# Token norm of a chunked scan: sums from one product with ones, and the power taken of 256 columns on every partition

## The chip, the cores and the metric

One core of one Trainium2 chip runs the program alone. The metric is the device time of one execution in microseconds (us), the median of several runs on the chip. A profiled execution gives the durations of single instructions.

## The reference, cut to what matters

The program is one residual layer of 256 tokens and 2048 channels: one input projection, a Mamba-2 scan and an attention branch on its results, two branch projections, a gated sum and an output projection. The part that the change touches is the gated group norm at the end of the scan branch. For each of 4 groups of 512 channels, with `y` the scan's output:

```python
y = y.reshape(bsz, L, SSM_D_INNER) * jax.nn.silu(z.astype(jnp.float32))
yg = y.reshape(bsz, L, SSM_GROUPS, -1)
yg = yg * lax.rsqrt(jnp.mean(yg * yg, axis=-1, keepdims=True) + EPS)
y = yg.reshape(bsz, L, SSM_D_INNER) * gn_m.astype(jnp.float32)
```

So each token has, in each group, one sum of squares over 512 channels, and one inverse root that scales all 512.

## The kernel before, in words

The projections keep TensorE busy. Their weights come in chunks of 1 MB: a DMA on SP's queue brings `raw`, ScalarE rounds it to `hi` (line 130), VectorE subtracts to get `lo` (line 131), and TensorE multiplies with both. Three chunks are held at once, and two are fetched ahead of the one in use (`next_chunk`): when TensorE begins chunk i, `hi` and `lo` of chunk i+2 are written into the buffers that chunk i-1 has just left. A chunk of the transposed kind (`chunk_t`, lines 159 and 164) is 16 products of 512 columns with `hi` and 16 of 256 columns with `lo`; within it two of the one kind and two of the other alternate, and the first product with `lo` stands third.

The scan works on channels as partitions and tokens as columns. Per group the program projects B and C, then x, then z (10 chunks), with the scan's own steps laid between the chunks by `after(n, fn)`, which runs `fn` n chunks later. The steps at the end of group g run during the first chunks of the next group, or, for the last group, during the projection of the indexer's queries:

- `mix` (lines 441 to 468) forms the gated output `yt` and, in `sz[:, 0, :]`, for each of 128 partitions the sum of 4 squares per token. The sum over the partitions is missing.
- `token_norm` (lines 470 to 481), two chunks later: TensorE takes each half of the squares as weights and a column of ones as the moving operand, which puts the sums of 128 tokens on 128 partitions, one column per half (`prs`, line 474). VectorE scales and adds the epsilon (line 476). GpSimd raises to the power -0.5 (line 477), on 128 partitions and 2 columns. ScalarE multiplies the identity with the two columns (line 480), which gives two diagonal matrices `dgy`.
- `normalised_y` (lines 483 to 496), two chunks after that: TensorE multiplies ones with the diagonals, which lays the factors along the columns on every partition (`prt`, line 487). VectorE multiplies four blocks of `yt` by the norm weight and by `prt` (line 490), ScalarE rounds to `yh`, VectorE subtracts to `yl`. The branch projection that reads `yh` and `yl` comes after the indexer.

The pool of small products in PSUM has 4 buffers (`aux_tile`). The pools `grp` and `grp2` of SBUF hold `dgy` in one buffer and `ss` in two. The order of the instructions on each engine is not the order of the source: the program's scheduler places them by readiness and priority, and each engine then executes its list strictly in order. `decay` (line 406) is the neighbour in time: lines 412, 418, 421 and 426 on VectorE, 409 and 410 on TensorE.

Of the kernel before, what the change touches and what calls it, by code (L numbers as in the profile page):

```python
# [11 lines left out]
F32 = mybir.dt.float32  # L12
F32R = mybir.dt.float32r
AF = mybir.ActivationFunctionType
ALU = mybir.AluOpType
# [3 lines left out]
P = 128  # L19
T = 256  # L20
D = 2048
KB = 16
EPS = 1e-6
# [9 lines left out]
PN, PCW, PCB, PGN, PDS, PDT, PAL = 0, 16, 112, 136, 152, 168, 169  # L33
# [51 lines left out]
def block_kernel(ctx, tc, W, w0, xT, xn, par, gbias, nf, out):  # L85
    nc = tc.nc
    mm = nc.tensor.matmul
# [14 lines left out]
    def aux_tile(shape, name):  # L102
        return paux.tile(shape, F32, tag="aux", name=name)
# [117 lines left out]
    part = const.tile([P, NPAR], F32, name="part")  # L221
    nc.sync.dma_start(part, par)
    ones = const.tile([P, P], F32, name="ones")
    nc.gpsimd.memset(ones, 1.0)
    mhalf = const.tile([P, 2], F32, name="mhalf")
    nc.gpsimd.memset(mhalf, -0.5)
    ident = const.tile([P, P], F32, name="ident")
# [17 lines left out]
    for k0, k1 in PIECES:  # L245
# [8 lines left out]
        for k in range(k0, k1):  # L254
            g = part[:, PN + k:PN + k + 1]
# [11 lines left out]
    grp = ssm.enter_context(tc.tile_pool(name="grp", bufs=1))  # L267
    grp2 = ssm.enter_context(tc.tile_pool(name="grp2", bufs=2))
# [200 lines left out]

    def token_norm(sz):  # L470

        prs = aux_tile([P, 2], "prs")
        for tb in range(2):
            mm(prs[:, tb:tb + 1], sz[:, 0, tb * P:tb * P + P], ones[:, 0:1], start=True, stop=True)
        ss = grp2.tile([P, 2], F32, tag="ss", name="ss")
        nc.vector.tensor_scalar(ss, prs, 1.0 / 512.0, EPS, ALU.mult, ALU.add)
        nc.gpsimd.tensor_tensor(ss, ss, mhalf[:, 0:2], op=ALU.pow)
        dgy = grp.tile([P, T], F32, tag="dgy", name="dgy")
        for tb in range(2):
            nc.scalar.activation(dgy[:, tb * P:tb * P + P], ident, AF.Copy, scale=ss[:, tb:tb + 1])  # L480
        return dgy

    def normalised_y(g, yt, dgy):
        prt = aux_tile([P, T], "prt")
        for tb in range(2):
            ts = slice(tb * P, tb * P + P)
            mm(prt[:, ts], ones, dgy[:, ts], start=True, stop=True)
        for b in range(4):
            k = 4 * g + b
            nc.vector.scalar_tensor_tensor(yt[:, b, :], yt[:, b, :], part[:, PGN + k:PGN + k + 1], prt,  # L490
                                           ALU.mult, ALU.mult)
        for a in range(2):
            bs = slice(2 * a, 2 * a + 2)
            ks = slice(4 * g + 2 * a, 4 * g + 2 * a + 2)
            nc.scalar.activation(yh[:, ks, :], yt[:, bs, :], AF.Copy)
            nc.vector.tensor_sub(yl[:, ks, :], yt[:, bs, :], yh[:, ks, :].bitcast(F32))
# [19 lines left out]
    for g in range(4):  # L516
# [17 lines left out]
        sz = grp.tile([P, 4, T], F32, tag="sz", name="sz")  # L534
# [8 lines left out]
        def finish(g=g, M=M, xdt=xdt, xss=xss, sz=sz):  # L543
            yt = mix(g, M, xdt, xss, sz)
            dgy = []
            after(2, lambda: dgy.append(token_norm(sz)))
            after(4, lambda: normalised_y(g, yt, dgy[0]))
# [304 lines left out]
```

## Time and profile before

| what | value |
|---|---|
| median of 3 runs | 1136.45 us (1135.76 to 1136.47) |
| the profiled execution's own time | 1137.44 us |
| its span, from the first to the last instruction | 1135.7 us |
| TensorE busy | 1124.4 us, 99% |
| VectorE busy | 779.5 us, 69% |
| ScalarE busy | 560.5 us, 49% |
| GpSimd busy | 8.8 us, 1% |
| mean granted TensorE clock | 0.999 |

The span and what lies around it (1.7 us) make the profiled time, which is 1.0 us above the median of the runs. Busy shares are averages over the span. A line of the timeline tells the start, the duration, the engine, the source line, the operation, what it writes and reads, and in brackets how long the engine had been idle and what ended that.

### The profile page before, as it was taken

To read this page: it belongs to the slowest core of one execution; us is meant where nothing else is said; L and a number is where in the kernel's file an instruction comes from. 1 tells how busy PE (TensorE), PEld (TensorE's weight loads), DVE (VectorE), ACT (ScalarE), POOL (GpSimd) and SP (SyncE) were. 2 spreads that over 40 slices of the span, in tenths; PEclk is the share of its full clock that TensorE was granted. 3 is DMA by queue.
4 is the path that set the end of the run, shared out by engine and by line. 5 is a ranking of instruction groups with operands and counts; after the bars stand their busy time and mean duration, and the time that the engine had idled before them with its cause. 6 is when DMAs were issued, how large, how long until landed. Compare 5 with 4: busy or idle time off the path is not lost.

```text
span 1135.7 us, 14327 instructions
## 1 busy us (share of the span) xinstructions
PE 1124.4 (99%) x5906; PEld 957.6 (84%) x5906; DVE 779.5 (69%) x995; ACT 560.5 (49%) x532; POOL 8.8 (1%) x24
## 2 busy tenths in 40 slices
PE   9999999999999999999999999999999999999997
PEld 8878888888888888888888888888888888888886
DVE  5788797879777854444447767876678454789663
ACT  6657574849454433334335454555445444333441
POOL 0000000000000000000000000000000000000000
PEclk9999999999999999999999999999999999999999
DMA  8766555563544655555554455445444557555652
GB/s 298 295 217 230 181 189 186 186 222 126 209 148 168 202 205 205 194 190 206 203 188 169 165 185 186 167 147 205 174 161 184 195 197 255 190 220 185 208 199 74
DMA packets 34113, 219.08 MB, mean 193 GB/s; under 512 B 3744, under 2 KB 3968, under 8 KB 9088
## 3 DMA queue, kind: packets, MB, share of 16 engines
q1 hardware_dynamic: 31248, 209.16, 51.9%
q10 hardware_dynamic: 2800, 9.01, 2.3%
q8 instruction: 46, 0.75, 0.3%
q14 instruction: 19, 0.16, 0.0%
HBM read 215.96 MB, written 2.13 MB: 192 GB/s over the span
## 4 chain that ended last, share of the span: by engine, by line
PE 94%; DMA 3%; DVE 2%; ACT 1%; SPq 0%; issue 0%; POOLq 0%; DVEq 0%; POOL 0%; ACTq 0%
PE acc_t L159 30%; PE acc_t L164 15%; PE acc_n L204 14%; PE acc_n L203 14%; PE acc_n L202 14%; DMA raw<-W 2%; PE py L454 1%; DVE lo L131 1%; PE acc_last L204 1%; PE acc_last L202 1%; PE acc_last L203 1%; PE pl L647 1%; PE po L675 1%; PE pi L564 1%; ACT hi L130 0%; DMA xt<-xn 0%
## 5 line engine op out<-in xcount | busy, mean ns | idle before, releaser
L131 DVE TENSOR_TENSOR lo<-raw,hi 128x2048 fp32r<-128x2048 f32 (+2 forms) x197 | 437.5, 2222 | 244.6 <-ACT hi L130 242.2
L130 ACT ACTIVATE hi<-raw 128x2048 fp32r<-128x2048 f32 (+2 forms) x197 | 366.4, 1861 | 446.1 <-PE acc_n L203 222.3
L159 PE MATMUL acc_t<-xx,hi 128*128 128x512 f32 x1472 | 466.7, 398 | 0.0
L164 PEld LDWEIGHTS acc_t<-xx,lo 128*128 128x128 f32 x1472 | 276.3, 188 | 65.2
L164 PE MATMUL acc_t<-xx,lo 128*128 128x256 f32 x1472 | 289.8, 278 | 0.0
L159 PEld LDWEIGHTS acc_t<-xx,hi 128*128 128x128 f32 x1472 | 224.9, 189 | 2.6 <-issue 1.7
L204 PE MATMUL acc_n<-lo,xx 128*128 128x512 f32 x480 | 187.0, 390 | 1.3 <-DVE lo L131 1.3
L202 PE MATMUL acc_n<-hi,xx 128*128 128x512 f32 x480 | 187.0, 390 | 0.0
L203 PE MATMUL acc_n<-hi,xx 128*128 128x512 f32 x480 | 186.9, 389 | 0.0
L204 PEld LDWEIGHTS acc_n<-lo,xx 128*128 128x128 f32 x480 | 90.1, 188 | 20.7 <-DVE lo L131 2.0
L203 PEld LDWEIGHTS acc_n<-hi,xx 128*128 128x128 f32 x480 | 90.1, 188 | 18.9 <-issue 0.3
L202 PEld LDWEIGHTS acc_n<-hi,xx 128*128 128x128 f32 x480 | 90.1, 188 | 18.5
L202 PE MATMUL acc_n<-hi,yh 128*128 128x512 f32 x256 | 99.6, 389 | 0.0
L203 PE MATMUL acc_n<-hi,yl 128*128 128x512 f32 x256 | 99.6, 389 | 0.0
L204 PE MATMUL acc_n<-lo,yh 128*128 128x512 f32 x256 | 99.6, 389 | 0.0
L202 PEld LDWEIGHTS acc_n<-hi,yh 128*128 128x128 f32 x256 | 48.0, 188 | 10.0
L204 PEld LDWEIGHTS acc_n<-lo,yh 128*128 128x128 f32 x256 | 48.0, 188 | 10.0
L203 PEld LDWEIGHTS acc_n<-hi,yl 128*128 128x128 f32 x256 | 48.0, 188 | 9.9
L667 DVE STREAM_TRANSPOSE pT<-le 32x192 f32<-32x192 f32 x128 | 47.3, 370 | 1.9
L401 DVE SCALAR_TENSOR_TENSOR c<-u,part,c 128x255 f32<-128x255 f32 (+2 forms) x72 | 30.2, 477 | 0.3
L726 DVE STREAM_TRANSPOSE mT<-merged 32x256 f32<-32x256 f32 x64 | 27.9, 436 | 0.8
L159 PE MATMUL acc_start<-xx,hi 128*128 128x512 f32 x64 | 17.7, 415 | 1.2 <-ACT hi L130 1.2
(198 smaller groups left out, 734.3 us busy)
## 6 DMA issues: line engine op xcount, KB each, us to landing
raw<-W SPq DMA_DIRECT2D x188, 1024.0 KB, 4.8
acb<-adr ACTq DMA_DIRECT2D x4, 1024.0 KB, 4.7
raw<-W SPq DMA_DIRECT2D x6, 512.0 KB, 7.4
xt<-xn SPq DMA_DIRECT2D x2, 1024.0 KB, 5.3
gb<-gbias SPq DMA_DIRECT2D x8, 256.0 KB, 3.5
xr<-xn ACTq DMA_DIRECT2D x4, 512.0 KB, 6.0
xraw<-xT SPq DMA_DIRECT2D x3, 512.0 KB, 6.5
raw<-W SPq DMA_DIRECT2D x4, 256.0 KB, 5.3
```

What stands on the lines that cost most here:

```text
L130: nc.scalar.activation(hi, raw, AF.Copy)
L131: nc.vector.tensor_sub(lo, raw, hi.bitcast(F32))
L159: mm(acc[:, cb, :], hv[:, k, cb], ax[:, kk].rearrange("p b t -> p (b t)"), start=kk == 0, stop=False, skip_group_check=True)
L164: mm(acc[:, cb, 0:T], lv[:, k, cb], ax[:, kk, 0, :], start=False, stop=kk == KB - 1, skip_group_check=True)
L202: mm(acc[:, c], ah[:, kk, ts], hv[:, k, c], start=kk == 0, stop=False)
L203: mm(acc[:, c], al[:, kk, ts], hv[:, k, c], start=False, stop=False)
L204: mm(acc[:, c], ah[:, kk, ts], lv[:, k, c], start=False, stop=kk == KB - 1)
L401: nc.vector.scalar_tensor_tensor(c[:, b, sh:], u[:, b, :T - sh], wv[3 - sh], c[:, b, sh:], ALU.mult, ALU.add)
L454: mm(py[r, cb, sb * P:], xdt[:, sb, 64 * h:64 * h + 64], M[a][:, 2 * cb + i, (0, T)[sb]:(T, 384)[sb]], start=cb == 0 and sb == 0, stop=cb ...
L564: mm(pi[2 * cb + i][:, cs[tb]], qi[r, cb, tb * P:tb * P + P], kidx[r, :(P, T)[tb]], start=tb == 0, stop=tb == 1, skip_group_check=True, ti ...
L667: nc.vector.transpose(t[sj, :, :, si], lv[si, :, :, sj])
L726: nc.vector.transpose(tv[sn, :, :, si], mv[si, :, :, sn])
```

## The change

`token_norm` multiplies ones, as weights, with the 256 columns of squares. That one product sums over the partitions and leaves every token's sum on every partition, along the columns, where `normalised_y` needs it. VectorE's scaling and GpSimd's power now run on 128 partitions and 256 columns; the exponent is one column, broadcast. The identity's two copies on ScalarE and the second product are gone, and `normalised_y` reads the factors from SBUF (`rs`) where it read them from PSUM (`prt`). `rs` takes the buffer that `dgy` had.

```diff
     def token_norm(sz):
 
-        prs = aux_tile([P, 2], "prs")
-        for tb in range(2):
-            mm(prs[:, tb:tb + 1], sz[:, 0, tb * P:tb * P + P], ones[:, 0:1], start=True, stop=True)
-        ss = grp2.tile([P, 2], F32, tag="ss", name="ss")
-        nc.vector.tensor_scalar(ss, prs, 1.0 / 512.0, EPS, ALU.mult, ALU.add)
-        nc.gpsimd.tensor_tensor(ss, ss, mhalf[:, 0:2], op=ALU.pow)
-        dgy = grp.tile([P, T], F32, tag="dgy", name="dgy")
-        for tb in range(2):
-            nc.scalar.activation(dgy[:, tb * P:tb * P + P], ident, AF.Copy, scale=ss[:, tb:tb + 1])
-        return dgy
-
-    def normalised_y(g, yt, dgy):
-        prt = aux_tile([P, T], "prt")
-        for tb in range(2):
-            ts = slice(tb * P, tb * P + P)
-            mm(prt[:, ts], ones, dgy[:, ts], start=True, stop=True)
+        prs = aux_tile([P, T], "prs")
+        mm(prs, ones, sz[:, 0, :], start=True, stop=True)
+        rs = grp.tile([P, T], F32, tag="dgy", name="rs")
+        nc.vector.tensor_scalar(rs, prs, 1.0 / 512.0, EPS, ALU.mult, ALU.add)
+        nc.gpsimd.tensor_tensor(rs, rs, mhalf[:, 0:1].to_broadcast([P, T]), op=ALU.pow)
+        return rs
+
+    def normalised_y(g, yt, rs):
         for b in range(4):
             k = 4 * g + b
-            nc.vector.scalar_tensor_tensor(yt[:, b, :], yt[:, b, :], part[:, PGN + k:PGN + k + 1], prt,
+            nc.vector.scalar_tensor_tensor(yt[:, b, :], yt[:, b, :], part[:, PGN + k:PGN + k + 1], rs,
                                            ALU.mult, ALU.mult)
```

## Rows read from the trace of the kernel before

**Rows 1.** The page: busy us (share of the span) and instructions of two engines.
```profile
PE 1124.4 (99%) x5906; PEld 957.6 (84%) x5906; DVE 779.5 (69%) x995; ACT 560.5 (49%) x532; POOL 8.8 (1%) x24
```

**Rows 2.** Windows, one group's period: length, then each engine's busy us, granted clock.
```profile
140.60:201.80 61.20, 61.20 (x374) 53.14 (x373) 51.10 (x63) 40.78 (x41) 1.11 (x2) 1.00 0.54 189
```

**Rows 3.** Timeline of PE around the two products of group 0.
```profile
137.52 0.62 PE L159 MATMUL acc_t<-xx,hi 128*128 128x512 f32 x2
...
138.22 0.50 PE L474 MATMUL prs<-ones,sz 128*128 128x1 f32 x4
...
139.36 0.62 PE L159 MATMUL acc_t<-xx,hi 128*128 128x512 f32 x2
...
150.49 0.61 PE L487 MATMUL prt<-dgy,ones 128*128 128x128 f32 x4
...
151.63 0.63 PE L159 MATMUL acc_t<-xx,hi 128*128 128x512 f32 x2
```

**Rows 4.** Timeline of PE: the nearest product of 256 float32 columns, with one of 128.
```profile
144.23 0.63 PE L159 MATMUL acc_t<-xx,hi 128*128 128x512 f32 x2
144.70 0.60 PE L409 MATMUL pcb<-bc 128*128 128x256 f32 x2
...
145.59 0.63 PE L159 MATMUL acc_t<-xx,hi 128*128 128x512 f32 x2
```

**Rows 5.** Groups of instructions on POOL: line, operation, shapes, count | busy us, mean ns.
```profile
L790 POOL TENSOR_TENSOR rf<-rf,mhalf 128x1 f32<-128x1 f32 x2 | 1.1, 550 | 0.2
...
L287 POOL TENSOR_TENSOR rn<-rn,mhalf 128x2 f32<-128x2 f32 x1 | 0.7, 717 | 0.1
...
L314 POOL MEMSET tri<- 128x384 f32 x1 | 0.4, 421 | 0.0
```

**Rows 6.** Timeline of POOL: the powers of groups 0, 2 and 3.
```profile
140.57 1.08 POOL L477 TENSOR_TENSOR ss<-ss,mhalf 128x2 f32<-128x2 f32 x1 [101.48 <-DVE ss L476]
...
263.01 1.00 POOL L477 TENSOR_TENSOR ss<-ss,mhalf 128x2 f32<-128x2 f32 x1 [60.19 <-DVE ss L476]
322.73 0.69 POOL L477 TENSOR_TENSOR ss<-ss,mhalf 128x2 f32<-128x2 f32 x1 [58.72 <-DVE ss L476]
```

**Rows 7.** Groups on DVE: the nearest operation of 256 columns out of PSUM.
```profile
L373 DVE COPY nat<-pn 128x256 f32<-128x256 f32 x1 | 0.4, 423 | 0.0
```

**Rows 8.** Timeline of DVE behind the scaling of group 0; last line, group 2.
```profile
140.34 0.15 DVE L476 TENSOR_SCALAR ss<-prs 128x2 f32<-128x2 f32 x1
140.41 0.68 DVE L421 TENSOR_TENSOR E<-acb,nat 128x512 f32<-128x512 f32 x1
142.24 2.29 DVE L131 TENSOR_TENSOR lo<-raw,hi 128x2048 fp32r<-128x2048 f32 x1 [1.15 <-ACT hi L130]
145.56 0.56 DVE L412 TENSOR_TENSOR cbt<-pcb,tri 128x384 f32<-128x384 f32 x1 [1.03 <-PE pcb L410]
...
151.13 0.48 DVE L490 SCALAR_TENSOR_TENSOR yt<-yt,part,prt 128x256 f32<-128x256 f32 x1
...
155.56 1.25 DVE L490 SCALAR_TENSOR_TENSOR yt<-yt,part,prt 128x256 f32<-128x256 f32 x3
156.74 2.28 DVE L131 TENSOR_TENSOR lo<-raw,hi 128x2048 fp32r<-128x2048 f32 x1
...
262.79 0.68 DVE L421 TENSOR_TENSOR E<-acb,nat 128x512 f32<-128x512 f32 x1
```

**Rows 9.** Timeline of PE: the first products of the chunk that uses that last `lo`.
```profile
162.44 0.71 PE L159 MATMUL acc_t<-xx,hi 128*128 128x512 f32 x2
```

**Rows 10.** Timeline of DVE behind the scaling of group 3.
```profile
323.72 2.29 DVE L131 TENSOR_TENSOR lo<-raw,hi 128x2048 fp32r<-128x2048 f32 x1 [1.14 <-ACT hi L130]
...
331.36 2.29 DVE L131 TENSOR_TENSOR lo<-raw,hi 128x2048 fp32r<-128x2048 f32 x1 [2.83 <-ACT hi L130]
...
334.28 0.69 DVE L194 TENSOR_TENSOR qi<-qi,rbc 128x512 f32<-128x512 f32 x1
```

**Rows 11.** Timeline of PE: the indexer's products that read that `qi`.
```profile
335.55 1.57 PE L564 MATMUL pi<-kidx,qi 64*128 64x128 f32 x12
```

## The prediction
> **What bounds the kernel now.** I read the page's busy times first: TensorE is busy 99% of the span, VectorE 69%, GpSimd 8.8 us in all [rows 1]. A share over the whole span hides stages, so I next took the windows of one group's period of the scan: in 61.2 us TensorE never pauses, at a granted clock of 1.00 (2.4 GHz), and VectorE works 51.1 us, 83% [rows 2]. Two things follow for the change. A TensorE instruction less in this stage is worth what it occupies there. And VectorE, which executes in order and writes the `lo` half of every weight chunk, has only some 10 us of play in 61: if it is held longer than its lead, TensorE stops. So the timelines of TensorE, GpSimd and VectorE around the norm come next.
>
> **What the change takes from TensorE.** The products with `lo` and `hi` alternate with a period of 0.70 us (137.52 to 138.22). Around `prs` the next period begins 1.14 us later instead (138.22 to 139.36), so the first product of the norm costs 0.44 us; around `prt` it is 150.49 to 151.63, again 0.44 us [rows 3]. Both go: 0.88 us per group. The new product is float32, 128x128 weights, 256 columns. The nearest rows are `pcb`: one product of 256 and one of 128 columns stretch a period from 0.70 to 1.36 us, 0.66 us for 384 columns, so 0.44 us for 256 [rows 4]. Ends: 0.12 us, if it streamed like the split products (0.70 us for 1536 columns), and 0.66 us. I take 0.44. The saving is 0.44 us per group, 1.8 us in four groups (0.9 to 3.0).
>
> **What it takes from ScalarE and adds to VectorE.** Eight identity copies leave ScalarE; TensorE has no pause that they end, so I cost that at nothing. VectorE's scaling grows from 0.15 to about 0.42 us, by the copy of 256 columns out of PSUM [rows 7, 8]; with lines 421 and 131 behind it, and 1.15 us idle before line 131 [rows 8], the 0.27 us disappear. The four products with the factor read SBUF for PSUM: same 256 columns, costed at nothing. PSUM's pool loses a tile per group: no wait. No DMA is added or moved.
>
> **What it adds to GpSimd.** This is the unknown. A power of one column takes 0.550 us, of two 0.717 or, in group 3, 0.69 [rows 5, 6]: the second column adds 0.14 to 0.17 us, about 0.153. If each column costs that, 256 take 0.70 + 254 x 0.153 = 39.6 us (36.0 to 43.1). Ends far away: below, 1.1 ns a column as for the memset of 384 columns in 0.42 us, which makes 1.0 us [rows 5]; above, 0.55 us for each column, 141 us. I take 39.6: it is the only pair of rows that shows this operation at two sizes.
>
> By the Trainium skill, GPSIMD Engine Reference, section 3.1 (elementwise, side by side), a two-input elementwise operation on GpSimd is bounded by its one read port at about 2.6 cycles an element of 1.2 GHz. By that page, as an estimate, 254 more columns would add 0.55 us, and the power would be hidden whole. The trace disagrees: the second column alone costs 0.14 us or more, some 60 times as much, so here the function, not the port, is the price.
>
> **Who waits for it.** Before, the power ran well ahead of its reader: it ended at 141.65, the first line 490 ran at 151.13 [rows 6, 8]. What follows on VectorE is the question. In group 0 the power took 1.08 us, and line 421 (two SBUF inputs) ran beside it until 141.09; in group 2 it took 1.00, with line 421 until 263.47. Both powers end 0.54 to 0.56 us after that operation. In group 3 VectorE was idle, and it took 0.69 [rows 6, 8, 10]. So the power waits for such a VectorE operation, and I take it that the exclusion works both ways: no operation with two SBUF inputs starts during a power. Line 131 is one. A second reason gives the same: the scheduler pulls ready work forward on VectorE (of four consecutive lines 490 one stands at 151.13, three at 155.56 [rows 8]), and without TensorE's `prt` ahead of them they are ready by dependency right behind the power, so one may sit in VectorE's list ahead of line 131.
>
> The Trainium skill's page SBUF — State Buffer, section "Who interferes with whom", says that GpSimd and VectorE share a port pair and that a VectorE instruction with two SBUF inputs contends with a GpSimd one that reads SBUF; whoever starts first holds it for the whole instruction. The rows agree in the one direction they show; the other no row shows. By the page VectorE stands still for the whole power; without that rule the sum would be rival A's.
>
> **The sum, groups 0 to 2.** Line 421 ends at 141.36 (0.27 later), the power 0.55 + 254 x 0.153 = 39.4 us after, at 180.8. The `lo` that started at 142.24 is frozen 38.6 us. Behind it VectorE has its list to work off. The `lo` that ended at 159.02 (156.74 + 2.28) is needed by the chunk whose products start at 162.44, after two products with `hi`, so at 162.9: 3.9 us lead [rows 8, 9]. The 1.03 us of idle time ahead of line 412 are filled too [rows 8]. TensorE loses 38.6 - 3.9 - 1.0 = 33.7 us per group. **Group 3:** the power runs alone from 323.0 to 362.6; the `lo` of 323.72 is frozen 38.9 us, and TensorE's products at 335.55 need the `qi` that VectorE finishes at 334.97. Of the 2.83 us idle ahead of the second `lo` ScalarE's rounding still takes most; I count 1.9 as filled: 37 us [rows 10, 11]. Loss: 3 x 33.7 + 37 = 138.1 us; with the saving, +136.3. On the profiled execution's 1137.44 us that is 1273.7; the median of the runs stands 1.0 lower, so 1272.7, and I say 1273.
>
> Slope 0.139 gives 14 us less, 0.167 14 us more: 1258 to 1287. TensorE's clock is 1.00 wherever the rows look, so none shows what a stop of 30 us does to it. A chunk of eight periods, 5.6 us, at the lower level would take 5.6 us more, at most 22 us in four stops; I cost it at nothing, because right after a stop VectorE's list sets the pace, and keep the end for the range.
>
> **Rival A, the cover holds (0.20).** Power as slow, but VectorE runs freely beside it and stops only at line 490, where that stands now. Then the hold is 151.13 to 180.8, 29.7 us, less the lead of 3.9: 25.8 per group; in group 3 from 335 to 362.6, less about 3.9: 23.7. Sum 101 - 1.8: 1236. For it: no VectorE operation with two inputs is seen waiting for a power. Against: the powers are seen waiting.
>
> **Rival B, the long loop is cheaper than its first columns (0.14).** If four columns are in flight together, 0.04 us a column makes 10.9 us: the freeze is 9.9 us, the loss 5.0 per group and 8 in group 3, +21: 1158. At 0.1 us a column the power takes 26 us, the freeze 25, the loss 3 x 20 + 23 - 1.8: 1218. So 1150 to 1220. Against: the second column does not come cheap behind the first.
>
> **Rival C, not slower (0.14).** The power ends before VectorE needs its result or the port. Either a column costs a few ns (the lower end), or nothing excludes VectorE and the lines 490 stand far enough back in its list; `yt`, which they scale, is only replaced a group's period later. The point from which it decides is 10 us of cover, about 40 ns a column, and 1 us if the port is held. Then only TensorE's saving is left: 1134.7, a gain of 0.16%. With the new product at its lower end, 3.0 us, 0.27%. For it: one column more is a thin sample of a loop of 256. Against: 0.14 us.
>
> A steeper slope than 0.167, up to the 141 us end (about 1680), keeps 0.04. The forecast has 0.48.
>
> **How the numbers follow.** The predicted time is the forecast's, 1273; its own range 1258 to 1295 with some of the clock. Range: forecast 0.48, rival A 0.20, rival B above 1160 0.11 give 0.79: 1160 to 1300. A measurement can tell about 0.2% (2.3 us) here. Slower by more: forecast, A, B, steeper, 0.86. Within: most of C, 0.11. Faster: C with the cheap product, 0.03.
>
> **What would show it.** GpSimd's busy time should rise from 8.8 us to about 160, in four powers of 36 to 43 us. VectorE should show one wait per group that ends with the power, ahead of a `lo` near 142 (forecast) or ahead of line 490 near 151 (rival A); TensorE should show idle time in four places of 30 us or more, released by line 131, and none elsewhere; its period around `prs` should be 1.14 us, with no `prt`. Powers under 10 us would make the forecast wrong at its first step; powers of 40 us without idle TensorE, at its second.

## The result and the profile after

The changed kernel takes 1289.44 us (4 runs, 1289.17 to 1290.37) against 1136.46 us: a ratio of 1.1347, 95% interval 1.1333 to 1.136. It is 153 us slower. The profiled execution took 1290.37 us, with a span of 1288.6 us.

Busy times and the clock line of the changed kernel's page; each digit of a row is the busy share, or the granted clock, of a slice of 32 us.

```profile
span 1288.6 us, 14270 instructions
...
PE 1131.8 (88%) x5882; PEld 961.2 (75%) x5882; DVE 780.4 (61%) x995; ACT 558.1 (43%) x524; POOL 170.4 (13%) x24
...
PE   8999629729719808999999999999999999999997
...
POOL 0000660660570570000000000000000000000000
PEclk9999959959959958999999999999999999999999
```

TensorE's busy time rose by only 7 us against [rows 1]; its share fell from 99% to 88%. So most of the loss is waiting. TensorE waits in four places, in the slices in which GpSimd works, and there the clock drops too. VectorE and ScalarE do about the same work as before.

The waits of the changed kernel, who waited for whom, total us, times, longest us:

```profile
DVE yt L482 <- POOL rs L476: 164.4, 4, 41.3
...
PE acc_t L164 <- DVE lo L131: 103.5, 4, 34.3
...
PE pi L556 <- DVE qi L194: 41.5, 1, 41.5
```

Line 476 is the power and line 482 the product with the factor (477 and 490 before). VectorE stands four times for the whole power, and TensorE for VectorE: three times 34 us (and once 0.5), and 41.5 us in group 3. That is 145 us of the 153; the rest comes from the clock, as shown below. In the chain that ended last GpSimd now holds 13%, where it had 0%.

The powers on GpSimd's timeline, and the same two places on VectorE's and TensorE's as in [rows 8] and [rows 3], all of the changed kernel:

```profile
140.25 41.53 POOL L476 TENSOR_TENSOR rs<-rs,mhalf 128x256 f32<-128x256 f32 x1 [100.76 <-DVE rs L475]
...
432.88 41.12 POOL L476 TENSOR_TENSOR rs<-rs,mhalf 128x256 f32<-128x256 f32 x1 [55.25 <-DVE rs L475]
```

```profile
139.75 0.42 DVE L475 TENSOR_SCALAR rs<-prs 128x256 f32<-128x256 f32 x1
140.08 0.68 DVE L421 TENSOR_TENSOR E<-acb,nat 128x512 f32<-128x512 f32 x1
181.81 0.88 DVE L482 SCALAR_TENSOR_TENSOR yt<-yt,part,rs 128x256 f32<-128x256 f32 x2 [41.05 <-POOL rs L476]
182.61 2.28 DVE L131 TENSOR_TENSOR lo<-raw,hi 128x2048 fp32r<-128x2048 f32 x1
```

```profile
136.95 0.63 PE L159 MATMUL acc_t<-xx,hi 128*128 128x512 f32 x2
...
137.65 0.59 PE L473 MATMUL prs<-sz,ones 128*128 128x256 f32 x2
...
138.77 0.63 PE L159 MATMUL acc_t<-xx,hi 128*128 128x512 f32 x2
...
149.97 0.63 PE L159 MATMUL acc_t<-xx,hi 128*128 128x512 f32 x2
184.95 0.80 PE L164 MATMUL acc_t<-xx,lo 128*128 128x256 f32 x2 [34.35 <-DVE lo L131]
185.54 1.05 PE L159 MATMUL acc_t<-xx,hi 128*128 128x512 f32 x2
...
189.19 0.62 PE L159 MATMUL acc_t<-xx,hi 128*128 128x512 f32 x2
```

Read from the bottom: TensorE stops in front of the first product with `lo` of a chunk. That `lo` starts on VectorE at 182.61. In [rows 8] it followed line 421; now two of lines 482 stand between, and the first of them waits for the power. In the order of the list, two of the four lines 482 were drawn ahead from behind the second `lo` to right behind line 421.

Windows of the changed kernel around the first stop; the columns are the stretch and its length, busy us of PE, PEld, DVE, ACT, POOL, then granted clock, DMA share and GB/s:

```profile
150.60:184.90 34.30, 0.00 (x0) 0.00 (x0) 3.09 (x4) 0.00 (x0) 31.18 (x1) 0.56 0.00 0
184.90:189.20 4.30, 4.25 (x15) 3.68 (x16) 4.26 (x7) 0.02 (x1) 0.00 (x0) 0.53 0.68 244
189.20:193.50 4.30, 3.83 (x23) 3.05 (x22) 4.30 (x4) 3.92 (x5) 0.00 (x0) 1.00 0.71 240
...
140.25:238.30 98.05, 63.24 (x368) 54.12 (x367) 51.31 (x63) 40.26 (x39) 41.54 (x2) 0.83 0.33 119
```

The last row is one group's period: 98.05 us in place of 61.20 [rows 2], with the same products on TensorE but for those of the norm. The granted clock fell in the stop and was still at the lower level, 1.2 GHz, in the 4.3 us behind it. ScalarE and the DMA are at 0 in the stop as well: the whole pipeline of weights stands while that one wait lasts.

### The profile page after: what moved, and what is told of

The parts are those of the page before. It is cut to its first block, busy times and chain, and to the rows that moved or that the text cites. A ratio compares the mean times of both kernels' runs of the same rounds, so it can differ in the third digit from the quotient of the medians.

```text
span 1288.6 us, 14270 instructions
## 1 busy us (share of the span) xinstructions
PE 1131.8 (88%) x5882; PEld 961.2 (75%) x5882; DVE 780.4 (61%) x995; ACT 558.1 (43%) x524; POOL 170.4 (13%) x24
## 4 chain that ended last, share of the span: by engine, by line
PE 76%; POOL 13%; DVE 7%; DMA 2%; ACT 1%; issue 1%; SPq 0%; POOLq 0%; DVEq 0%; ACTq 0%
PE acc_t L159 23%; POOL rs L476 13%; PE acc_n L204 12%; PE acc_n L203 12%; PE acc_n L202 12%; PE acc_t L164 11%; DVE lo L131 3%; DMA raw<-W 2%; DVE c L401 1%; ACT hi L130 1%; PE acc_last L204 1%; PE acc_last L203 1%; PE acc_last L202 1%; PE py L454 1%; PE pl L639 1%
## 5 line engine op out<-in xcount | busy, mean ns | idle before, releaser
L159 PE MATMUL acc_t<-xx,hi 128*128 128x512 f32 x1472 | 472.5, 403 | 0.0
L164 PEld LDWEIGHTS acc_t<-xx,lo 128*128 128x128 f32 x1472 | 280.1, 191 | 172.0 <-DVE lo L131 105.6
L164 PE MATMUL acc_t<-xx,lo 128*128 128x256 f32 x1472 | 293.6, 281 | 103.5 <-DVE lo L131 103.5
L159 PEld LDWEIGHTS acc_t<-xx,hi 128*128 128x128 f32 x1472 | 228.6, 192 | 2.7 <-issue 1.7
L476 POOL TENSOR_TENSOR rs<-rs,mhalf 128x256 f32<-128x256 f32 x4 | 165.5, 41378 | 269.0 <-DVE rs L475 269.0
L482 DVE SCALAR_TENSOR_TENSOR yt<-yt,part,rs 128x256 f32<-128x256 f32 x16 | 7.3, 480 | 164.4 <-POOL rs L476 164.4
L398 ACT ACTIVATE c<-u,part 128x256 f32<-128x256 f32 x24 | 13.2, 594 | 121.9 <-DVE u L395 121.8
```

The costliest lines, as they stand in the source:

```text
L159: mm(acc[:, cb, :], hv[:, k, cb], ax[:, kk].rearrange("p b t -> p (b t)"), start=kk == 0, stop=False, skip_group_check=True)
L164: mm(acc[:, cb, 0:T], lv[:, k, cb], ax[:, kk, 0, :], start=False, stop=kk == KB - 1, skip_group_check=True)
L398: nc.scalar.activation(c[:, b, :], u[:, b, :], AF.Identity, bias=part[:, PCB + blk:PCB + blk + 1], scale=wv[3])
L476: nc.gpsimd.tensor_tensor(rs, rs, mhalf[:, 0:1].to_broadcast([P, T]), op=ALU.pow)
```

## The experiments

Two theories stood against each other. T: a column of the power costs 0.16 us, and the loss comes from where its reader stands in VectorE's list. L, the first of the prediction's two reasons for VectorE's stop: a running power keeps out every VectorE operation with two SBUF inputs, so the loss would come wherever the reader stood.

**Everything but the power.** The changed kernel, with

```diff
-        nc.gpsimd.tensor_tensor(rs, rs, mhalf[:, 0:1].to_broadcast([P, T]), op=ALU.pow)
+        nc.gpsimd.tensor_tensor(rs[:, 0:2], rs[:, 0:2], mhalf[:, 0:2], op=ALU.pow)
```

> The power is taken of 2 of the 256 columns; the other columns are multiplied with the mean square itself, so the norm is left out for them. All else is the changed kernel. Theory T (the loss is the length of the power times its place in VectorE's list) and rival L (a running power keeps out every VectorE operation with two SBUF inputs) agree: a power of about 0.7 us, VectorE's wait ahead of line 482 under 1.5 us, no idle TensorE in the scan, and only the saving of the two products left: before less 1.8 us, 1134.7 us (1133.5 to 1136). If the time stays over 1140, something other than the power is slow.

Measured: 1135.34 us, ratio 0.9988 (0.9979 to 0.9997). The powers take 0.69 to 1.08 us as before. So the product with ones, the longer scaling on VectorE and the reader in SBUF together gain about 1 us of the 1.8 expected, at the edge of what can be told. One part of the expectation missed: TensorE does stop in the scan, for 1.1 us in group 3. All of the loss of 153 us is the power's. The page, VectorE's timeline in group 0 and TensorE's in group 3:

```profile
PE 1121.3 (99%) x5882; PEld 954.2 (84%) x5882; DVE 780.8 (69%) x995; ACT 558.6 (49%) x524; POOL 8.7 (1%) x24
```

```profile
140.29 0.68 DVE L421 TENSOR_TENSOR E<-acb,nat 128x512 f32<-128x512 f32 x1
141.57 0.88 DVE L482 SCALAR_TENSOR_TENSOR yt<-yt,part,rs 128x256 f32<-128x256 f32 x2 [0.60 <-POOL rs L476]
142.37 2.29 DVE L131 TENSOR_TENSOR lo<-raw,hi 128x2048 fp32r<-128x2048 f32 x1
```

```profile
334.75 1.58 PE L556 MATMUL pi<-kidx,qi 64*128 64x128 f32 x16 [1.12 <-DVE qi L194]
```

VectorE's list is the changed kernel's: two of lines 482 stand right behind line 421 with a power of 2 columns as with one of 256.

**A long power that nobody reads.** The kernel before, with one line behind line 477 (`base` is a constant tile of 0.7, `spare` a tile of its own):

```diff
         nc.gpsimd.tensor_tensor(ss, ss, mhalf[:, 0:2], op=ALU.pow)
+        nc.gpsimd.tensor_tensor(spare, base, ss[:, 0:1].to_broadcast([P, T]), op=ALU.pow)
```

> The kernel before, with one more power per group on GpSimd, right behind the one of 2 columns: 256 columns into a tile that nobody reads. Nothing waits for its result, so it shows whether a long power holds VectorE by itself. T: the power takes 38 to 45 us, VectorE runs on beside it, and the time is that of before, 1136.5 us (1135 to 1139). L: the lo of each group near 142, 203, 265 and 324 us is frozen to the end of the power, TensorE stops four times for 30 us or more, 1255 to 1290 us.

Measured: 1136.76 us, ratio 1.0002 (0.9992 to 1.0011): nothing lost, with 41 us of power in each group. Its timelines of GpSimd and of VectorE, and a window over the power:

```profile
140.37 41.13 POOL L481 TENSOR_TENSOR spare<-base,ss 128x256 f32<-128x256 f32 x1
```

```profile
140.88 2.29 DVE L131 TENSOR_TENSOR lo<-raw,hi 128x2048 fp32r<-128x2048 f32 x1 [1.14 <-ACT hi L130]
...
145.27 1.75 DVE L429 TENSOR_TENSOR E<-E,cbt 128x1536 f32<-128x1536 f32 x1
...
147.54 2.29 DVE L131 TENSOR_TENSOR lo<-raw,hi 128x2048 fp32r<-128x2048 f32 x1
```

```profile
140.60:182.00 41.40, 41.40 (x244) 36.37 (x243) 34.33 (x37) 28.00 (x29) 40.91 (x1) 1.00 0.57 205
```

The `lo` of 140.88 starts half a microsecond into the power, and 34 us of VectorE's work, lines 131 and 429 with their two SBUF inputs among it, lie beside it, at the durations of before (2.29 us a `lo`, in [rows 8] 2.28 and 2.29). The power is no longer for it either: 41.13 us here, 41.12 in group 3 of the changed kernel, where VectorE stood still. L is refuted.

**The same power, its reader late.** The changed kernel, with

```diff
     def normalised_y(g, yt, rs):
+        prt = aux_tile([P, T], "prt")
+        mm(prt, ident, rs, start=True, stop=True)
...
-            after(4, lambda: normalised_y(g, yt, dgy[0]))
+            after(10, lambda: normalised_y(g, yt, dgy[0]))
```

and `prt` for `rs` in the four products.

> The changed kernel with its power of 256 columns, but its reader comes late: normalised_y runs 10 chunks behind mix instead of 4, and reads the factors through a product with the identity, so that nothing of it can be drawn ahead on VectorE. T: the powers still take 41 us each, all of it beside VectorE and TensorE; the product added is worth the 0.44 us per group that the change saved, so 1136.5 us (1134 to 1140, some waiting where the late steps meet the next mix). L: as slow as the changed kernel, 1270 to 1290 us, with line 131 waiting for GpSimd.

Measured: 1135.96 us, ratio 0.9997 (0.9988 to 1.0006). The powers still take 41 us; the scaling ahead of them stands where it did, and the reader now runs 45 us behind it. Group 0, GpSimd's timeline and VectorE's:

```profile
139.94 41.52 POOL L476 TENSOR_TENSOR rs<-rs,mhalf 128x256 f32<-128x256 f32 x1 [101.27 <-DVE rs L475]
```

```profile
139.77 0.69 DVE L421 TENSOR_TENSOR E<-acb,nat 128x512 f32<-128x512 f32 x1
141.34 2.29 DVE L131 TENSOR_TENSOR lo<-raw,hi 128x2048 fp32r<-128x2048 f32 x1 [0.87 <-ACT hi L130]
...
184.64 1.66 DVE L484 SCALAR_TENSOR_TENSOR yt<-yt,part,prt 128x256 f32<-128x256 f32 x4 [1.08 <-PE prt L481]
```

With the reader out of the way the same power costs nothing. That undoes the 153 us, with a power as long as before (41.52 us, 41.53 in the changed kernel).

**The reader late in the source only.** As the last, with `after(10, ...)` but without the product: the factors are read from `rs`.

```diff
-            after(4, lambda: normalised_y(g, yt, dgy[0]))
+            after(10, lambda: normalised_y(g, yt, dgy[0]))
```

> The changed kernel with normalised_y 10 chunks behind mix instead of 4, the factors still read from SBUF directly, without the product with the identity. If the place in the source decided, VectorE would not meet the power any more: 1135 us. T says the list decides: the scheduler draws lines 482 ahead to the scaling again, since nothing but the power stands before them, and the time is that of the changed kernel, 1280 to 1295 us, with two of lines 482 right behind line 421.

Measured: 1288.89 us, ratio 1.1342 (1.1327 to 1.1358), as slow as the changed kernel. Its timeline of VectorE:

```profile
139.60 0.67 DVE L421 TENSOR_TENSOR E<-acb,nat 128x512 f32<-128x512 f32 x1
181.32 0.88 DVE L482 SCALAR_TENSOR_TENSOR yt<-yt,part,rs 128x256 f32<-128x256 f32 x2 [41.05 <-POOL rs L476]
182.12 2.28 DVE L131 TENSOR_TENSOR lo<-raw,hi 128x2048 fp32r<-128x2048 f32 x1
```

The list has not changed at that place: ten chunks in the source in place of four do not move the readers. The two runs with ten chunks differ only in the product, so the product made the difference between them. That the product `prt` alone kept lines 490 back in the kernel before is argued, not shown: the long power with the product and four chunks was not run, and there TensorE itself could stand in front of the product.

**Shorter powers.** The changed kernel with the power of 32, and of 64, of the columns:

```diff
+        nc.gpsimd.tensor_tensor(rs[:, 0:32], rs[:, 0:32], mhalf[:, 0:1].to_broadcast([P, 32]), op=ALU.pow)
```

> The changed kernel with the power of 32 of the 256 columns (the norm is left out for the rest). T: at 0.16 us a column the power takes 5.7 us. Its first reader stands ahead of a lo that has some 7 us of lead (in the changed kernel's list, two of lines 482 and the lo take 3.0 us between the power's end and the point where TensorE went on, and TensorE stopped 10.4 us behind the power's start), so groups 0 to 2 hide it; in group 3 VectorE's list up to the indexer's qi has about 4 us of idle time, so up to 3 us are lost: 1135 to 1140 us. If a power of any length costs its full length, 1157 us.

> The changed kernel with the power of 64 of the 256 columns (the norm is left out for the rest). T: the power takes 10.8 us; less the lead of 7.3 us it stops TensorE for 3 to 5 us in groups 0 to 2 and for 6 to 11 us in group 3: 1150 to 1162 us. A price per instruction instead of per column would leave 1135 us; a price that is not linear in the columns would show in the power's own time.

Measured: 1146.46 us (ratio 1.0089, 1.0075 to 1.0103) and 1167.76 us (1.028, 1.0264 to 1.0297). Both are above what was expected, by 6 us. Group 3's powers, which start beside an idle VectorE, take 5.42 and 10.52 us, and 41.12 with 256 columns: 0.159 us a column from 32 to 64 and from 64 to 256 alike. The price per column is right and linear. TensorE's stops, with 32 columns (group 0, group 3) and with 64 (group 0, two; then the waits of the whole run):

```profile
156.85 0.50 PE L164 MATMUL acc_t<-xx,lo 128*128 128x256 f32 x2 [1.21 <-DVE lo L131]
...
343.18 2.93 PE L556 MATMUL pi<-kidx,qi 64*128 64x128 f32 x16 [5.84 <-DVE qi L194]
```

```profile
154.53 0.80 PE L164 MATMUL acc_t<-xx,lo 128*128 128x256 f32 x2 [3.76 <-DVE lo L131]
...
162.65 0.50 PE L164 MATMUL acc_t<-xx,lo 128*128 128x256 f32 x2 [0.84 <-DVE lo L131]
```

```profile
PE acc_t L164 <- DVE lo L131: 15.0, 6, 3.8
PE pi L556 <- DVE qi L194: 10.9, 1, 10.9
```

With 32 columns the first `lo` behind the power is in time and the second is not: some 6 us of other VectorE work stand between them, two lines 426 and two lines 482 among it. That second `lo` was not in the expectation. In group 3 no slack is left at all: a power of 5.42 us stops TensorE for 5.84, where up to 3 us were expected. With 64 columns the stops are 5.0 us per group in groups 0 to 2 and 10.9 in group 3, both at the top of what was expected but inside it. What the expectation left out there is the clock behind the stops: TensorE is busy 1128.3 us, and 1121.3 with two columns, for the same products, so 7 us (2.8 us with 32 columns). From 64 to 256 columns the time rises by 121.7 us, 30.4 per group, and the power by 30.6: over this stretch every microsecond of power is a microsecond of time.

**Another root.** The changed kernel with ScalarE's square root and VectorE's reciprocal:

```diff
-        nc.gpsimd.tensor_tensor(rs, rs, mhalf[:, 0:1].to_broadcast([P, T]), op=ALU.pow)
+        nc.scalar.activation(rs, rs, AF.Sqrt)
+        nc.vector.reciprocal(rs, rs)
```

> The changed kernel with the power replaced: ScalarE's square root of the 256 columns and VectorE's reciprocal. T: the product with ones keeps its saving, the root (0.4 us and a table load of 1.3) and the reciprocal (about 1.75 us, as the one of 256 columns on line 335) hide: 1134.7 us (1133.5 to 1137). The rival here: ScalarE and VectorE are too full behind the scaling, a lo comes late, and the time is 1137 to 1142 us.

Measured: 1134.48 us (11 runs, 1133.88 to 1135.18), ratio 0.9983 (0.9974 to 0.9992): 1.9 us faster than the kernel before, and as forecast. The page and the timelines of ScalarE and VectorE:

```profile
PE 1120.6 (99%) x5882; PEld 953.3 (84%) x5882; DVE 786.6 (69%) x999; ACT 564.9 (50%) x532; POOL 4.9 (0%) x20
```

```profile
143.49 1.28 ACT L476 ACT_TABLE_LOAD   x1
144.78 0.42 ACT L476 ACTIVATE rs<-rs 128x256 f32<-128x256 f32 x1
```

```profile
141.55 2.29 DVE L131 TENSOR_TENSOR lo<-raw,hi 128x2048 fp32r<-128x2048 f32 x1 [0.88 <-ACT hi L130]
...
146.75 1.75 DVE L477 RECIPROCAL rs<-rs 128x256 f32<-128x256 f32 x1
...
153.42 0.88 DVE L483 SCALAR_TENSOR_TENSOR yt<-yt,part,rs 128x256 f32<-128x256 f32 x2
```

Some 3.5 us per group on ScalarE and VectorE replace 41 on GpSimd, and TensorE keeps its 99%. The readers (here line 483) moved too: without any `prt` they stand behind the first two `lo`, with the reciprocal ahead of them in VectorE's own list, and TensorE does not stop in group 3. So this run changes the length of the root and the place of its readers together; the run with two columns shows that a short power alone already undoes the loss.

## Why the prediction was right, and where not

The direction and the size were right: the forecast was 1273, its own range reached 1295. The chain (a slow power holds VectorE, a `lo` comes late, TensorE stops) was right, but of the two reasons for VectorE's stop one was wrong, and errors of the sum cancel in part. Step by step, on the spans (1288.6 - 1135.7 = +152.9 us, where the sum said +136.3):

- **TensorE's saving.** The period around `prs` is 138.77 - 136.95 = 1.82 us where two take 1.40, so the product costs 0.42 us (0.44 forecast), and `prt` is gone. That part was right: the run with another root gains 1.9 us where 1.8 were forecast. The run with two columns gains 1.1; its stop of 1.1 us in group 3 is about the difference.
- **The power.** 41.12 us where VectorE is idle against 39.6, and 41.0 behind the end of line 421 (140.76 to 181.78) against 39.4. The slope read off one and two columns was 0.139 to 0.167, taken as 0.153; it is 0.159. This term is short by 1.5 to 1.6 us per group, 6 us in all.
- **Who waits.** Two reasons were given for VectorE's stop. The second, that lines 482 are drawn ahead of the `lo`, is what happens. The first, that the exclusion between GpSimd and an operation with two SBUF inputs works both ways, is wrong: the run with an unread power shows 34 us of VectorE's work beside 41 us of power. What the rows of before showed [rows 6, 8] is real and small: a power that starts while line 421 runs takes 0.3 to 0.4 us more (41.53, 41.43 and 41.43 against 41.12 here). The Trainium skill's page SBUF — State Buffer, section "Who interferes with whom", by which the pair is held for the whole instruction, disagrees with this run; the measurement decides. The sum came out near since the wrong reason and the right one stop VectorE at nearly the same place: it froze the `lo` of 142.24, and in the changed kernel the wait stands just ahead of that `lo`, at line 482. For the first reason that is luck.
- **The lead.** The forecast took 3.9 us of lead from the third `lo` and 1.0 us of idle time, 33.7 us lost per group. In the new list the first `lo` decides (34.35 us, then 0.47 at the second). The place was wrong; the loss came within 1 us, with 1.6 us more of power in it, so the lead was taken 1 us too small.
- **Group 3.** 37 us forecast; 41.5 measured. 1.5 of the difference is the power; for the rest, the four lines 482 and two lines 488 now stand ahead of the `qi` in VectorE's list, which the sum left out: before, lines 490 ran at 335.66, behind the `qi` of [rows 10].
- **The clock.** Costed at nothing behind a stop, because VectorE would set the pace. That step failed: VectorE delays TensorE by only 0.47 us there, while in the 4.3 us at 1.2 GHz three periods take 3.65 us (185.54 to 189.19) for 2.1, and the start 0.36 more: 1.9 us. Read in the same way, the stops of groups 1, 2 and 3 cost 2.4, 2.9 and 2.8 us. That is 10 us in all, inside the 22 us kept for the range. TensorE's busy time says the same: 1131.8 us, and 1121.3 for the same products in the run with two columns.

Power 6, clock 10 and group 3 some 3 us, less 2 at the lead, are the 17 us between sum and result. Rival A (VectorE free until line 490 stands where it stood) has its premise confirmed and its place refuted: VectorE is free beside a power, but the line moved. Rival B (the loop cheaper than its first columns) is excluded by the power's 41 us and the equal slopes. Rival C needs what the run with the late reader provides, and there the time is not slower: 1135.96 us.

## What to carry to other kernels

A small operation on an idle engine has its price per element: read it off two sizes in the trace before giving it 128 times the columns, since an idle engine's length counts as soon as a full engine waits for it in order. Where an instruction of such an engine's list needs a slow result, what matters is its place in the list. Here the scheduler put the readers at the same early place for a power of 2 columns and of 256; a later place in the source alone did not move them, and with a product ahead of them it did. Whether redundant columns are cheap depends on the engine that works them off: the same root of 256 columns costs 1.28 us of table load, 0.42 and 1.75 us on ScalarE and VectorE, and 41 on GpSimd. And a stop costs more than its length: here 2 to 3 us more behind each long one, at the lower clock.

## What the runs showed of the hardware that was not expected

A power on GpSimd takes 0.159 us a column of 128 partitions, linear from 32 to 256 columns. A power that starts while VectorE's line 421 (two SBUF inputs) runs takes 0.3 to 0.4 us more; whether the two inputs are the cause, no run tells. VectorE operations with two SBUF inputs that start while a power runs are not delayed (2.29 us for a `lo` either way). TensorE's granted clock was near the lower level, 1.2 GHz, behind a stop of 3.76 us (0.57) as behind the long ones (0.53 in group 0). Behind that shorter stop of the run with 64 columns the windows read:

```profile
154.50:158.20 3.70, 3.67 (x13) 3.19 (x14) 3.67 (x6) 0.00 (x0) 0.00 (x0) 0.57 0.77 241
158.20:162.00 3.80, 3.61 (x21) 2.81 (x19) 3.80 (x3) 3.24 (x5) 0.00 (x0) 1.00 0.70 276
```

Behind a stop of 1.21 us (32 columns, group 0) the next period takes 0.71 us, the full rate.
